# Even-layer input projections of two token groups by seven half-size products, and the forward gated pass as two streams

## The chip, the core and the metric

The kernel runs on one core of one Trainium2 chip. Its engines are TensorE (PE, matrix products into PSUM), VectorE (DVE), ScalarE (ACT), GpSimd (POOL) and SyncE (SP), which here issues all DMA transfers. The metric is device microseconds of the whole program, as the median of several executions; smaller is better. One further execution is recorded by the hardware profiler, and all rows shown come from it.

## What is computed

A two-layer encoder over 2048 prompt tokens and 512 sample tokens, width 1024, in float32. The even layer projects its input once, and two mixers share the projection: gated linear attention (four heads, one scan in each direction, decays that depend on the data) and window attention (eight query heads, two key heads, a bias by distance, a sink logit). The odd layer is a gated convolution of width three. Cut to what matters here:

```python
def even_sublayer(x, w_in, w_up_f, b_f, w_up_b, b_b, norm_g, sink, rel_bias, w_out):
    u = x @ w_in
    qa, ka, va, za, gd, qb, kb, vb, zb = jnp.split(u, _offsets(EVEN_SPLITS), axis=-1)
    ya = gla_mixer(qa, ka, va, za, gd, w_up_f, b_f, w_up_b, b_b, norm_g)
    yb = swa_mixer(qb, kb, vb, zb, rel_bias, sink)
    return jnp.concatenate([ya, yb], axis=-1) @ w_out
...
        x = layer_norm(DN_ALPHA * x + sub, ln_g[l], ln_b[l])
```

## The kernel before

**Precision.** A float32 product is made of three products of a reduced type: every operand is split into a high part and the rest, and high x high, high x rest and rest x high are summed in PSUM. ACT makes the high part with a cast; the rest is a subtraction, on DVE for activations (`prep`, L795) and on POOL for weights (`cook`, `cook_low`, L531 and L545).

**Tiles and stages.** The 2560 tokens form five groups of 512, group 4 being the sample and groups 0 to 3 the prompt; each group holds four chunks of 128. In the even layer's input projection 21 channel tiles of 128 (k: 0 to 3, q: 4 to 7, keys and queries of window attention: 8 to 12, the gates: 13 to 20) are computed per group by `dense_ch` (L569), 24 matmuls of 512 columns each: eight slices of the contraction, three products. Values and the low-rank input of the decays come from `e1_tok` (L1025), 192 matmuls of 336 columns. `e1_ch` (L1071) runs the channel tiles and hands each PSUM bank to `take`, which scales, splits or gates it and stores it to DRAM; for tiles 2 to 9 it also makes one decay each way per head (one matmul, then four functions on ACT and one DVE instruction). The list `stages` in `run` (L2103) fixes the order of the dense work: token projections and channel tiles of group 4, of 3, of 2, of 1, the output projection of group 4 (oe4), then group 0, the odd layer's input projection of group 4 (`odd_one`, called "one"), output projections oe0, oo4, oe1, oe2, and two "pair" stages of the odd layer.

**A stage of seven products exists already.** `odd_pair` (L1944) treats two groups and two channel tiles as a 2 x 2 block product and makes it of seven products of half the contraction (12 matmuls of 512 columns each) rather than eight. `prep_pair` (L909) makes the sums of activation blocks, `pair_weights` (L1858) the sums of weight blocks, and the results are sums of the seven banks, made on DVE.

**Two streams run beside the dense work.** `gla_stream` (L1454) goes through the groups 4, 3, 2, 1, 0. For each chunk `inside` (L1186) does the work within the chunk and the backward scan; when a sequence is through (after group 4, and after group 0) `along` (L1402) makes the forward pass, one step per chunk, each step with its state update, norm, transposes and store. `swa_front` (L1510) and `swa_back` (L1579) do window attention, one block per chunk: scores, bias and softmax in front, products with the values behind. `setup_bias` (L734) loads its bias into two of the four tiles P. A mark such as `gla_in3` or `swa_in3` in `flow.done` tells a stream that a group's inputs are stored; `done_e1_0` says that all of group 0's are. `best` in `swa_front` takes the newest group first, and from `done_e1_0` on the lowest chunk first (L1523).

**The order is written out ahead.** `Flow` and `Model` (L97 and L263) go through the program with estimated times; the dense list drives, and at each pause `pump` (L337) issues the steps of the streams whose data should be ready. Streams have a rank (preparation 0, gated 1, window 2), and `room` (L332) holds them back while DVE or ACT is over 4 or 5 us behind PE by the estimate. Each engine then works through its queue in this fixed order. Where the dense list needs a mark that is not there, `until` (L346) lets the streams go on alone. The output projection of group g waits so, in `out_ln` (L1758), for its `prep`, which waits for `gla`g and for the four blocks of window attention of the group (`mixed`, L2125).

**Tiles.** `st` are eight tiles of 128 x 4 x 512 for split activations (four for a group); `wh`, `wl`, `ws` belong to the weights; `md` (8) and `pr` (3) are general tiles of 128 x 512; P, Q, K0, K1, V, pth, ptl and gb are window attention's; tA, tB, QQ, KK, A, S, km, qn, v are gated attention's. Profile rows give all work the same line, L242, because a helper records it; so tiles tell groups apart.

Of the kernel before, what the change touches and what calls it, by code (L numbers as in the profile page):

```python
# [376 lines left out]
class Trunk:  # L377
    def __init__(self, tc, nc, I, y_out, ctx):
# [35 lines left out]
        self.blocks = []  # L414
# [319 lines left out]
    def setup_bias(self):  # L734
        nc, I, c = self.nc, self.I, self.const
        yield from self.setup_late()
        oh = self.e((32, 512), "gb", bufs=2)
        nc.sync.dma_start(oh[:], I["onehot"])
        ml = self.e((8, 512), "gb", bufs=2)
# [6 lines left out]
        line = self.e((8, 512), "pth", bufs=2)  # L746
# [4 lines left out]
        for h in range(8):  # L751
            rows = self.e((128, 512), "ptl", bufs=2)
            nc.sync.dma_start(rows[:], self.line_s[h:h + 1].broadcast_to([128, 512]))
            yield [rows]
            nc.sync.dma_start(self.bias_s[h], rows[:])
            yield 2.0
        b = self.bias_s
        yield 6.0
        self.bias = [self.new(self.e2, (128, 4, 385), F32, "P", 4, True) for _ in range(2)]
# [265 lines left out]
    def e1_tok(self, g):  # L1025
# [9 lines left out]
        stores = {"gla_in": 24, "swa_in": 29, "done_sw": 33, "done_e1_": 37}  # L1035
# [35 lines left out]
    def e1_ch(self, groups, us):  # L1071
# [3 lines left out]
        if us[0] == 0:  # L1075
            if groups == (4,):
# [25 lines left out]
        def split(g, u, p):  # L1102
            sc = 1.0 if u == 8 else 0.125
            hi, lo = self.m2(dt=F32R), self.m2(dt=F32R)
# [6 lines left out]
            def store():  # L1111
                for i, o in enumerate((hi, lo)):
                    for hh in range(2):
# [4 lines left out]
                        else:  # L1118
                            nc.sync.dma_start(
                                self.qb_s[4 * g:4 * g + 4, 64 * i:64 * i + 64, 2 * (u - 9) + hh].rearrange("c p t -> p c t"),  # L1120
                                s.rearrange("p (c t) -> p c t", c=4))
                self.left[g]("swa_in")
            flow.defer(rest, hi, lo, p)

        def take(g, u, p):
            if u < 8:
# [7 lines left out]
                if u == 0:  # L1134
# [3 lines left out]
                    X = G[g] = self.new(self.yp, (128, 512), F32R, "y", 4, True)  # L1138
# [12 lines left out]
            if 1 < u < 10:  # L1151
                decay(g, (u - 2) // 4, (u - 2) % 4)

        for u in us:
# [7 lines left out]
            if u == 9:  # L1162
                self.drop(up, *(G[g] for g in groups))
                up = self.up = None
                G.clear()
        if u == 16:
            for g in groups:
                self.release("e1_%d" % g)
                flow.mark("end_e1_%d" % g)

# [15 lines left out]
    def inside(self, c, first, last, ld, K, ahead):  # L1186
# [189 lines left out]
        if not last:  # L1376
# [4 lines left out]
            self.flow.defer(lambda: nc.sync.dma_start(self.m_s[c], A[:].rearrange("p h t -> p (h t)")), A)  # L1381
        yield [Q]

    def along_load(self, c, first, last):

        nc = self.nc
        X = self.e((128, 2, 512), ("tA", "QQ")[c % 2])
        nc.sync.dma_start(X[:, 1], self.op_s[c])
        if not first:
            nc.sync.dma_start(X[:, 0], self.qf_s[c])  # L1390
        if c % 2:
            M = None if last else self.e((128, 512), "v")[:]
            ga = self.e((128, 512), "qn")[:]
        else:
            Y = self.e((128, 2, 512), "KK")
            M, ga = Y[:, 0], Y[:, 1]
        if not last:
            nc.sync.dma_start(M, self.m_s[c])
        nc.sync.dma_start(ga, self.ga_s[c])
        return X, M, ga  # L1400
# [804 lines left out]
```

## Time and profile before

| | us |
|---|---|
| median of three runs | 2368.8 |
| lowest and highest of them | 2368.19, 2370.43 |
| the profiled execution | 2370.12 |
| its span, first to last instruction | 2368.1 |

The granted PE clock over the span was 0.998 of full speed. The stages, by their first matmul on PE in the trace: token projections of group 4 from 6.4 us, its channel tiles from 40, group 3 from 165 and 203, group 2 from 372 and 413, group 1 from 587 and 629, oe4 from 804, group 0 from 866 and 902, "one" from 1075, oe0 from 1320, the two pair stages from 1506 and 1914. The span is what lies between the first and the last instruction; the measured time of the same execution is 2.0 us longer. A row by stretches gives, for each engine, its busy time and, behind the x, the number of its instructions. Because matmuls are pipelined, a busy PE says that matmuls were in flight; how many ran in a stretch says how fast.

### The profile page before, as it was taken

Reading aid. Unit: us, or ns where it says so; the run is one execution under the profiler, and the core shown is the slowest. Engines: PE = TensorE matmul, PEld = TensorE weight load, DVE = VectorE, ACT = ScalarE, POOL = GpSimd, SP = SyncE. Lnnn points to the kernel's source line nnn. Section 1 sums busy time; section 2 is a strip of 40 time slices with the busy share of each in tenths; the row PEclk is TensorE's granted clock in tenths of the full one; section 3 lists DMA queues with packets and bytes.
Section 4 is the critical chain, followed back from the end, with each engine's and each line's share of the span. In section 5 each row is a group of like instructions: output and inputs, shape, how many; then the busy total and the mean of one; then the engine's idle time right before and its main releaser. Section 6 shows DMA issues by size and latency. Waiting matters only on the chain.

```text
span 2368.1 us, 43087 instructions
## 1 busy us (share of the span) xinstructions
PE 2343.9 (99%) x15830; PEld 1951.8 (82%) x15830; DVE 1582.8 (67%) x2699; ACT 1226.1 (52%) x2363; POOL 1418.4 (60%) x1610
## 2 busy tenths in 40 slices
PE   8999999999999999999999999999999999999998
PEld 8888889888988888888888888878888877888887
DVE  2267756767767677577776467876566587656567
ACT  4666776656576645665577532543334343333431
POOL 5454435443444444444444467898887689988674
PEclk9999999999999999999999999999999999999999
DMA  7977686676667657675478777232124633221573
GB/s 230 295 226 233 221 269 229 209 221 221 218 194 236 223 173 242 197 218 161 158 245 268 266 261 243 92 116 89 52 78 140 217 105 103 73 72 58 175 242 121
DMA packets 275057, 437.37 MB, mean 185 GB/s; under 512 B 21360, under 2 KB 160240, under 8 KB 274848
## 3 DMA queue, kind: packets, MB, share of 16 engines
q1 hardware_dynamic: 274848, 434.64, 56.5%
q8 instruction: 125, 2.05, 0.4%
q14 instruction: 84, 0.69, 0.1%
HBM read 319.72 MB, written 114.84 MB: 184 GB/s over the span
## 4 chain that ended last, share of the span: by engine, by line
PE 87%; DVE 5%; POOL 4%; DMA 2%; issue 1%; ACT 1%; SPq 0%; POOLq 0%; DVEq 0%; ACTq 0%
PE acc L242 71%; PE ps L242 17%; POOL wl L242 1%; POOL wh L242 1%; DVE st L242 1%; DVE bst L242 1%; DVE y L242 1%; POOL md L242 0%; SPq L242 0%; DVE QQ L242 0%; DVE P L242 0%; DVE KK L242 0%; DMA K<-kb_s 0%; DMA mix_s<-gb 0%; DMA op_s<-QQ 0%
## 5 line engine op out<-in xcount | busy, mean ns | idle before, releaser
L242 POOL TENSOR_TENSOR wl<-ws,wh 128x256 fp32r<-128x256 f32 (+1 forms) x912 | 750.7, 855 | 711.4 <-PE acc L242 478.0
L242 PE MATMUL acc<-st,wh 128*128 128x512 f32 x3160 | 828.5, 395 | 2.8 <-DVE pr L242 2.0
L242 PEld LDWEIGHTS acc<-st,wh 128*128 128x128 f32 x3160 | 580.9, 188 | 121.0 <-issue 3.1
L242 PE MATMUL acc<-st,wl 128*128 128x512 f32 x1744 | 471.9, 395 | 2.8 <-POOL wl L242 1.9
L242 PE MATMUL acc<-wh,st 128*128 128x512 f32 (+1 forms) x1680 | 389.4, 371 | 7.9 <-ACT st L242 6.4
L242 PEld LDWEIGHTS acc<-st,wl 128*128 128x128 f32 x1744 | 320.8, 188 | 68.0 <-POOL wl L242 4.1
L242 PEld LDWEIGHTS acc<-wh,st 128*128 128x128 f32 x1680 | 300.2, 189 | 55.1 <-ACT st L242 6.4
L242 ACT CAST wh<-ws 128x1024 fp32r<-128x1024 f32 (+2 forms) x252 | 249.0, 989 | 184.2 <-DMA ws<-in_w_oo 55.9
L242 PE MATMUL acc<-wl,st 128*128 128x512 f32 (+1 forms) x840 | 209.0, 368 | 0.6 <-POOL wl L242 0.5
L242 ACT ACTIVATE md<-md 128x512 f32<-128x512 f32 x264 | 164.7, 631 | 20.5 <-DVE md L242 14.9
L242 PEld LDWEIGHTS acc<-wl,st 128*128 128x128 f32 x840 | 150.7, 188 | 23.8 <-POOL wl L242 1.3
L242 DVE SCALAR_TENSOR_TENSOR md<-acc,md 128x512 f32<-128x512 f32 (+1 forms) x113 | 77.0, 683 | 81.5 <-ACT md L242 76.5
L242 DVE TENSOR_TENSOR st<-pr,st 128x512 fp32r<-128x512 f32 x115 | 98.5, 874 | 41.6 <-ACT st L242 41.2
L242 ACT ACTIVATE md<-acc 128x512 f32<-128x512 f32 (+1 forms) x133 | 76.2, 597 | 67.0 <-PE acc L242 66.5
L242 POOL TENSOR_TENSOR wh<-md,wh 128x256 fp32r<-128x256 f32 x118 | 96.7, 842 | 13.6 <-ACT wh L242 13.1
L242 ACT CAST pth<-ps 128x512 fp32r<-128x512 f32 x112 | 65.3, 583 | 73.1 <-PE ps L242 72.3
L242 DVE CUSTOM_DVE_ANT_0 P<-ps,P 128x384 f32<-128x384 f32 (+1 forms) x160 | 79.3, 525 | 29.6 <-PE ps L242 29.0
L242 ACT ACTIVATE P<-P,nm 128x385 f32<-128x385 f32 (+1 forms) x160 | 93.2, 587 | 3.9 <-DVE nm L242 3.9
L242 ACT ACTIVATE mv<-mv,eps 128x1 f32<-128x1 f32 x40 | 11.8, 295 | 151.8 <-DVE mv L242 147.7
L242 PE MATMUL acc<-P,wh 128*128 128x512 f32 x312 | 89.5, 400 | 0.4 <-POOL wh L242 0.4
L242 ACT COPY km<-KK 128x512 f32<-128x512 f32 x80 | 50.8, 635 | 72.2 <-DVE KK L242 50.9
L242 ACT CAST st<-pr 128x512 fp32r<-128x512 f32 x115 | 68.3, 617 | 30.3 <-DMA pr<-mix_s 12.9
(490 smaller groups left out, 4090.2 us busy)
## 6 DMA issues: line engine op xcount, KB each, us to landing
ws<-in_w_ch SPq DMA_DIRECT2D x105, 512.0 KB, 4.4
ws<-in_w_od SPq DMA_DIRECT2D x58, 512.0 KB, 4.2
ws<-in_w_oe SPq DMA_DIRECT2D x40, 512.0 KB, 3.8
ws<-in_w_oo SPq DMA_DIRECT2D x36, 512.0 KB, 3.5
K<-kb_s SPq DMA_DIRECT2D x32, 384.0 KB, 6.3
d_s<-md SPq DMA_DIRECT2D x40, 256.0 KB, 4.2
qb_s<-md SPq DMA_DIRECT2D x80, 128.0 KB, 3.9
tA<-d_s SPq DMA_DIRECT2D x20, 512.0 KB, 5.7
```

Source lines behind the costliest of these rows:

```text
L242: r = f(*a, **k)
```

## The change

Groups 4 and 3 are projected together. The order becomes: token projections of both, channel tile 0 of both, then ten units of two channel tiles by `even_pair`, with `prep_even` for the activations' blocks (raw inputs loaded again, four block sums, three of them kept in window attention's tiles and in `md`) and `pair_weights` for the weights' blocks. The decays are made in the first four units; the queries of window attention come in the seventh and eighth unit. The gated stream starts when the tiles that it shares are free ("early", after four units); the bias is loaded after the last unit has released P. The forward pass becomes two streams: `along` makes the output and the next state, `along_back` the norm, transposes, gate and store, up to three chunks behind. All other stages stay.

```diff
         nc, I, c = self.nc, self.I, self.const
         yield from self.setup_late()
-        oh = self.e((32, 512), "gb", bufs=2)
+        yield "up"
+        yield 2.0
+        oh = self.e((32, 512), "QQ")
         nc.sync.dma_start(oh[:], I["onehot"])
-        ml = self.e((8, 512), "gb", bufs=2)
+        ml = self.e((8, 512), "tA")
         nc.sync.dma_start(ml[:], I["mline"])
...
+        for i in (6, 7, 5):
+            yield "free_paire_%d" % i
+        while self.free_at([(self.e2, "P", 4)]) > self.flow.t:
+            yield 0.4
         self.bias = [self.new(self.e2, (128, 4, 385), F32, "P", 4, True) for _ in range(2)]
...
-        stores = {"gla_in": 24, "swa_in": 29, "done_sw": 33, "done_e1_": 37}
+        names = ["gla_in", "swa_in", "done_sw", "done_e1_"] if g < 3 else ["gla_in", "done_e1_", "swa_in", "done_sw"]
+        stores = {n: 24 + sum({"swa_in": 5}.get(x, 4) for x in names[1:i + 1]) for i, n in enumerate(names)}
...
-                    X = G[g] = self.new(self.yp, (128, 512), F32R, "y", 4, True)
+                    X = G[g] = self.take([(self.e2, "v", 1), (self.e2, "qn", 1)] if units else [(self.yp, "y", 4)],
+                                         (128, 512), F32R)
...
+        if units:
+            own = self.owned["e1_%d" % groups[1]]
+            self.drop(*own[:2])
+            del own[:2]
+            flow.mark("plain_e")
+            yield from self.even_pair(groups, units, take, put, decay)
...
+    def prep_even(self, a, b):
+
+        nc, flow = self.nc, self.flow
+        yield "start_e1_%d" % a
+        yield 20.0
+        hi, lo = {}, {}
+        self.pairs["e"] = (hi, lo)
+        e2 = self.e2
+        self.rooms = {n: m for n, m in (("P", 3), ("Q", 2))}
+        homes = [(e2, "P", 4), (e2, "Q", 1), (e2, "pth", 2), (e2, "ptl", 2), (e2, "gb", 2), (e2, "K0", 1), (e2, "K1", 1),
+                 (e2, "V", 1), (self.md, "md", 8)]
...
+        for n in (6, 7, 5):
+            hi[n], lo[n] = [], []
+        self.early = early = [(e2, "S", 2), (e2, "km", 2), (e2, "A", 1), (e2, "tB", 1)]
+        places = early + self.half
+        todo, raws, last = [(k, i, g) for k in range(4) for i in range(2) for g in (a, b)], [], []
...
+        for k in range(4):
+            while len(raws) < 4:
+                get()
+                if len(raws) < 4:
+                    yield 0.4
+            yield raws[:4]
+            while self.free_at(places) > flow.t:
+                yield 0.4
+            b11, b12, b21, b22 = raws
+            t = self.take(places, (128, 512))
+            sub(t[:], b12[:], b11[:])
+            sub(b12[:], b22[:], b12[:])
+            sub(b22[:], b22[:], t[:])
+            sub(b21[:], b21[:], b22[:])
+            self.drop(b11)
+            last.append(b21)
+            raws.clear()
+            yield [b22]
+            for n, r in ((6, b22), (7, b12), (5, t)):
+                hi[n].append(cell())
+                lo[n].append(cell())
+                split(n, k, r, None)
+                yield []
+        yield "plain_e"
+        hi[4], lo[4] = self.big_cells(), self.big_cells()
+        for k, r in enumerate(last):
+            split(4, k, r, None)
+            yield []
+
...
+    def even_pair(self, groups, units, take, put, decay):
+
+        nc, flow = self.nc, self.flow
+        a, b = groups
+        hi, lo = self.pairs["e"]
+        at = lambda c: c[0][:, c[1]]
+        H, L = {}, {}
+        for i, g, o in ((1, a, 0), (2, a, 4), (3, b, 4)):
+            H[i], L[i] = ([f(o + k) for k in range(4)] for f in self.x["e1_%d" % g])
...
+        def after(i, u):
+            c1, c2 = u["ct"]
+            if i == 1:
+                u["s1"] = mid()
+                nc.scalar.copy(u["s1"][:], u[1][:])
+            elif i == 6:
+                flow.force(u[1])
+                u["u1"] = mid()
+                add(u["u1"], u[6], u["s1"])
+            elif i == 7:
+                flow.force(u[6])
+                u["u2"] = mid()
+                add(u["u2"], u[7], u["u1"])
+            elif i == 5:
+                flow.force(u[6])
+                flow.force(u[7])
+                t = mid()
+                add(t, u[5], u["u2"])
+                out(b, c2, t)
+                add(u["u1"], u[5], u["u1"])
+            elif i == 2:
+                flow.force(u[5])
+                t = mid()
+                add(t, u[2], u["s1"])
+                out(a, c1, t)
+                self.drop(u["s1"])
+            elif i == 4:
+                flow.force(u[2])
+                add(u["u2"], u[4], u["u2"])
+                out(a, c2, u["u2"])
+            else:
+                flow.force(u[5])
+                flow.force(u[4])
+                add(u["u1"], u[3], u["u1"])
+                out(b, c1, u["u1"])
+            self.drop(u[i])
+
+        decays = [(g, i // 4, i % 4) for i in range(8) for g in groups]
+        end = len(units) - 1
+        for n, cts in enumerate(units):
+            u = {"ct": cts}
+            for i in (1, 6, 7, 5, 2, 4, 3):
+                if n == 0 and i in (4, 5, 6, 7):
+                    yield "paire_%d" % i
+                if (n, i) == (end - 1, 1):
+                    flow.mark("late_paire")
+                if "wb_e_%d_%d" % (n, i) not in flow.done:
+                    yield "wb_e_%d_%d" % (n, i)
+                if i not in H:
+                    H[i], L[i] = [at(c) for c in hi[i]], [at(c) for c in lo[i]]
+                w = self.wblocks.pop(("e", n, i))
+                p = u[i] = self.pd(hold=True)
+                for k in range(4):
+                    c = slice(k * 128, k * 128 + 128)
+                    nc.tensor.matmul(p[:], w[:, 0, c], H[i][k], start=(k == 0), stop=False)
+                    nc.tensor.matmul(p[:], w[:, 0, c], L[i][k], start=False, stop=False)
+                    yield
+                for k in range(4):
+                    c = slice(k * 128, k * 128 + 128)
+                    nc.tensor.matmul(p[:], w[:, 1, c], H[i][k], start=False, stop=(k == 3))
+                    if k == 1:
+                        yield
+                self.drop(w)
+                flow.defer(lambda i=i, u=u: after(i, u), p)
...
+                if n < 4 and i in (6, 5, 2, 3) and decays:
+                    decay(*decays.pop(0))
+                yield
+            if n == 3:
+                self.drop(self.up, *(self.G[g] for g in groups))
+                self.up = None
+                self.G.clear()
+                flow.mark("early")
+        del self.pairs["e"]
...
+        self.backs.append((c, X))
...
+    def along_back(self):
+        for c in [*range(16, 20), *range(16)]:
+            while not self.backs:
+                yield 0.4
+            _, X = self.backs.pop(0)
+            yield [X]
...
+            if g == 4:
+                yield "early"
+                while any(self.model.spare(*h[1:]) < h[2] for h in self.early + [(self.e2, "qn", 1), (self.e2, "v", 1)]):
+                    yield 0.4
...
+            front, back = {}, {}
+            todo = [list(range(c0, c1)) for _ in range(2)]
+
+            def more(c):
+                if todo[0] and todo[0][0] <= c + 1:
+                    x = todo[0].pop(0)
+                    front[x] = self.along_load(x, *ends(x))
+                x = todo[1][0] if todo[1] else c1
+                if x <= c + 2 and x < c1 and (x < c0 + 3 or "back_%d" % (x - 3) in self.flow.done):
+                    back[x] = self.along_load_back(todo[1].pop(0))
+            more(c0 - 1)
+            for c in range(c0, c1):
+                more(c)
+                while c not in back:
+                    yield 0.4
+                    more(c)
+                ld, X = front.pop(c), back.pop(c)
+                yield [x for x in (*ld, X) if x is not None]
+                yield from self.along(c, *ends(c), ld, X)
+                ld = X = None
             self.sf = None
+            yield "back_%d" % (c1 - 1)
...
-                while self.free_at(self.mids) > flow.t:
+                places = self.mids if p != "e" or n == 0 else self.half + (self.early if n < 4 else self.large)
+                while self.free_at(places) > flow.t:
                     yield 0.3
-                t = sums[name] = self.take(self.mids, (128, 512))
...
-        stages = [("tok", 4), ("ch", ((4,), A + B)), ("tok", 3), ("ch", ((3,), A + B)),
+        even = [(1, 2), (3, 4), (5, 6), (7, 8), (13, 14), (15, 16), (9, 10), (11, 12), (17, 18), (19, 20)]
+        stages = [("tok", 4), ("tok", 3), ("ch", ((4, 3), [0], even)),
...
-        flow.add(self.prep("e1_3", xT(3), ["start_e1_4"]), 60.0, True)
-        flow.add(self.prep("e1_2", xT(2), ["start_e1_3"], then="end_e1_4"), 150.0, True)
-        flow.add(self.prep("e1_1", xT(1), ["start_e1_2"], then="end_e1_3"), 150.0, True)
+        flow.add(self.prep("e1_3", xT(3), ["start_e1_4"], deep=3), 4.0, True)
+        flow.add(self.prep("e1_2", xT(2), ["late_paire"], then="free_paire_1"), 150.0, True)
+        flow.add(self.prep("e1_1", xT(1), ["start_e1_2"]), 150.0, True)
...
+        flow.add(self.pair_weights("e", [tuple(I["w_ch"][u] for u in x) for x in even], 0), 0.0, True)
+        flow.add(self.prep_even(4, 3), 0.0, True)
...
+        flow.add(self.along_back(), rank=1)
```

## What is predicted, before the changed kernel has run

> **What bounds the kernel now.** I read the page's busy times first, then the waits of TensorE (PE), then busy time in stretches cut at the stages. The first fence holds the page's busy line and two of its 40-slice rows, then one line of the view of waits.
>
> ```profile
> PE 2343.9 (99%) x15830; PEld 1951.8 (82%) x15830; DVE 1582.8 (67%) x2699; ACT 1226.1 (52%) x2363; POOL 1418.4 (60%) x1610
> PE   8999999999999999999999999999999999999998
> DVE  2267756767767677577776467876566587656567
> ...
> PE acc L242 <- ACT st L242: 6.4, 1, 6.4
> ```
>
> PE is busy almost everywhere and its one long wait, 6.4 us, is the start. VectorE (DVE) sits near seven tenths from slice 3 to slice 22, where the two attention streams run beside the projections. The next fence is the view by stretches (busy us and instructions of PE, weight loads, DVE, ACT, POOL; granted clock; DMA share and rate).
>
> ```profile
> 0.00:43.00 43.00, 36.40 (x207) 34.11 (x208) 15.52 (x31) 17.23 (x30) 25.52 (x44) 1.00 0.72 230
> 43.00:166.00 123.00, 123.00 (x782) 100.87 (x781) 45.37 (x82) 76.38 (x124) 61.46 (x82) 1.00 0.87 270
> 43.00:366.00 323.00, 323.00 (x2522) 272.12 (x2521) 179.90 (x389) 216.68 (x438) 150.90 (x197) 1.00 0.78 246
> 366.00:475.00 109.00, 108.91 (x1165) 94.01 (x1164) 81.16 (x174) 69.61 (x136) 48.31 (x65) 1.00 0.69 220
> 475.00:527.00 52.00, 52.00 (x588) 42.02 (x587) 38.30 (x76) 31.06 (x56) 26.88 (x30) 1.00 0.73 217
> 527.00:965.00 438.00, 436.85 (x4088) 369.99 (x4088) 315.94 (x663) 264.00 (x519) 189.81 (x244) 1.00 0.67 215
> 965.00:1017.00 52.00, 52.00 (x381) 42.94 (x380) 27.40 (x55) 32.15 (x58) 23.18 (x30) 1.00 0.71 209
> 1017.00:1200.00 183.00, 182.38 (x1692) 149.73 (x1691) 140.56 (x294) 106.70 (x213) 82.77 (x95) 1.00 0.58 186
> 1200.00:1319.00 119.00, 119.00 (x616) 100.44 (x615) 78.50 (x151) 85.68 (x260) 52.17 (x67) 1.00 0.79 261
> 1319.00:1413.00 94.00, 93.83 (x434) 77.77 (x433) 50.63 (x71) 36.36 (x83) 55.42 (x66) 1.00 0.75 259
> 1500.00:1600.00 100.00, 97.00 (x412) 77.67 (x411) 81.40 (x95) 41.97 (x73) 92.28 (x86) 0.98 0.26 90
> 1550.00:1555.00 5.00, 4.07 (x11) 2.93 (x10) 3.93 (x7) 2.34 (x3) 5.00 (x7) 0.66 0.26 105
> 1600.00:1700.00 100.00, 100.00 (x439) 81.98 (x438) 61.29 (x77) 36.52 (x53) 87.81 (x92) 1.00 0.24 79
> ```
>
> From 1600 to 1700 nothing but 512-wide matmuls runs: 100/439 = 0.2278 us each. So the kernel is bound by PE's count of matmuls, as long as the streams arrive in time. How near they are to being late is in the next fence: issues from the views by tile, and one line of the DMA queue's timeline.
>
> ```profile
> L242 SPq DMA_DIRECT2D P<-bias_s x2: 426/467/508, 126.2 to 126.6; - x2
> L242 SPq DMA_DIRECT2D Q<-qb_s x20: 319/332/593, 132.4 to 1186.9; - x20
> L242 SPq DMA_DIRECT2D KK<-k_s x40: 319/423/1602, 109.5 to 1130.7; - x40
> L242 SPq DMA_DIRECT2D mix_s<-gb x20: 524/565/826, 235.8 to 1261.1; - x20
> L242 SPq DMA_DIRECT2D mix_s<-qn x10: 524/525/847, 334.1 to 1358.4; - x10
> 1263.46 1.60 SPq L242 DMA_DIRECT2D pr<-mix_s  x3
> 1319.65 1.17 PE L242 MATMUL acc<-wh,st 128*128 128x512 f32 x4
> ```
>
> Window attention starts 6 us after its bias is loaded, loads its 20 blocks from 132 to 1187, and stores the last at 1261. The output projection of group 0 (oe0) loads its input 2 us later and begins on PE at 1319.7. So its slack is some 50 us. The gated stream's last forward steps (1358) are wanted only by a much later stage.
>
> **The matmuls.** Twenty channel tiles of two groups took 20 x 2 x 24 = 960 matmuls; ten units of seven products of 12 take 840. 120 x 0.2278 = **27.3 us less**. The 21st tile and the token products stay.
>
> **What the units need from the other engines** is priced by these groups of the view by shape.
>
> ```profile
> L242 DVE TENSOR_TENSOR md<-acc,md 128x512 f32<-128x512 f32 x91 | 61.1, 681 | 13.4 <-PE acc L242 11.3 <-ACT md L242 1.3
> L242 DVE TENSOR_TENSOR md<-md,ws 128x512 f32<-128x512 f32 x11 | 13.7, 1244 | 13.0 <-POOL md L242 13.0
> L242 ACT CAST wh<-md 128x512 fp32r<-128x512 f32 x59 | 36.4, 619 | 90.5 <-PE acc L242 41.4 <-DVE md L242 39.2 <-POOL md L242 9.9
> L242 ACT ACTIVATE md<-md 128x512 f32<-128x512 f32 x264 | 164.7, 631 | 20.5 <-DVE md L242 14.9
> L242 POOL TENSOR_TENSOR wl<-md,wl 128x256 fp32r<-128x256 f32 x74 | 60.5, 840 | 5.1 <-ACT wl L242 5.1
> L242 DVE TENSOR_TENSOR st<-pr,st 128x512 fp32r<-128x512 f32 x115 | 98.5, 874 | 41.6 <-ACT st L242 41.2
> ```
>
> A unit lasts 7 x 12 x 0.2278 = 19.1 us on PE. Beside it run: on DVE seven additions, 7 x 0.681 = 4.8 us; on ACT seven casts, 7 x 0.619 = 4.3 us, one copy of about 0.6, and in the first four units four decays of four functions, 16 x 0.63 = 10 us; on POOL 14 subtractions, 14 x 0.84 = 11.8 us, and up to four sums of weights at about 1.24. All fit in 19 us, though POOL reaches 17. The block sums for the activations (prep_even) cost 16 subtractions, 16 casts and 16 more subtractions: 32 x 0.874 = 28 us of DVE, over the first 95 us, where DVE was a third busy (43 to 166: 45 of 123). SiLU and the splits now read both inputs from SBUF, 42 DVE instructions at up to 1.244 instead of 0.681, 24 us at the most, in the same light stretch. I cost all this at nothing; the cover is PE's own 19 us a unit. Twenty weight tiles of 512 KB are loaded once less, 16 inputs of 256 KB once more, all through SP: nothing, at a DMA share that falls from 0.87.
>
> **Friction.** The first difference of weights needs two sums, a cast and two subtractions (2 x 1.24 + 0.62 + 1.68 = 4.8 us) against a slot of 12 x 0.2278 = 2.7 us. The old seven-product stage lost (439 - 412) x 0.228 = 6.2 us in its first 100 us, with DVE at 81%. Bounds 0 and 6.2; DVE is lighter here, so 3. Group 3's token stage moves up to about 43 us, when its input must be split already, and group 2's activations wait for the last unit's buffers: bounds 0 and the 6.4 of the old start; nearer 0, since the loads go on beside a whole stage, so 1. Together **4 us**.
>
> **What moves, and the stall it may bring.** This term decides the sign. The tiles of window attention (P, Q, K0, K1, V, pth, ptl, gb) now hold block sums until the last unit, and the bias is loaded only then. When is that? Start and first token stage 43; the second, 192 of the first's matmuls, 192/207 x 36.4 = 34, so 77; tile 0 for both groups 48 x 0.2278 = 11, so 88; 840 matmuls 191, decays 4, friction 3, so 286. Gated attention starts after four units (about 183) and adds PE time: between 43 and 366 all but 1008 x 0.2278 + 34 + 4 = 268 us was streams', 55 us for four chunks and some four blocks, 7 us each; about 3.3 chunks fit, 23 us. The stage ends near 309 and window attention starts near **315 instead of 132**. Its DVE time by tile (P, ptl, gb in turn; columns as above):
>
> ```profile
> 43.00:366.00 323.00, 12.69 (x84) 10.19 (x84) 34.68 (x76) 25.21 (x90) 0.00 (x0) 1.00 0.78 246
> 366.00:1319.00 953.00, 54.55 (x364) 44.80 (x364) 116.92 (x244) 79.40 (x270) 0.00 (x0) 1.00 0.68 215
> 43.00:366.00 323.00, 7.88 (x20) 3.79 (x20) 13.63 (x20) 0.00 (x0) 1.00 0.78 246
> 43.00:366.00 323.00, 0.00 (x0) 0.00 (x0) 5.48 (x8) 4.65 (x8) 5.66 (x4) 1.00 0.78 246
> ```
>
> By 366, where the old group 3 is done, 34.7 + 13.6 + 5.5 = 54 us of it were over; the new kernel has done none. Gated attention is behind by about half a chunk and four forward steps, some 20 us of DVE (an estimate: a chunk each 45 us at two fifths of DVE is 18). To be done from 315 until the output projection of group 1 (oe1), for which all blocks of groups 0 and 1 are wanted: the old 366 to 1413, 81 + 38 + 316 + 27 + 141 + 79 + 51 = 733, plus 54 + 20 = **807 us**. Without a stall oe1 comes at 1413 - 23 = 1390, 1075 us later: DVE must be **75.1%** busy. With both streams at work it was 81.2/109 = 74.5% (366 to 475), 315.9/438 = 72.1% (527 to 965), 140.6/183 = 76.8% (1017 to 1200). At 76.8% the work takes 1051 us and nothing waits; at 74.5% 1083, **8 us late**; at 72.1% 1119, 44 late. Below zero the term can't go, since PE has its matmuls to do. I take 74.5%, the row nearest to what is needed. The waiting instruction is the first matmul of oe0 or oe1 (dense stream, at out_ln); behind it stand all dense matmuls, while the streams' own go on.
>
> The two-stream forward pass changes no instruction's size; it lets a step's state update run ahead of its norms. Its end gates nothing before (1358 against a stage beyond 1750), so 0; it is cover for the later start of the gated stream (183 against 110), which has the tiles to itself until 315 and so catches up.
>
> **Sum**: -27.3 + 4 + 8 = -15.3 us. Against the profiled execution (span 2368.1, 2370.1 with what lies around it, and 2368.8 the median, 0.7 over the span) that is 2352.8 of span and **2353.5** on the medians' scale.
>
> **A rule on the clock.** In the row 1550 to 1555 the granted clock was 0.66 and 11 matmuls took 4.07 us of busy time, where full rate gives 18: 7 x 0.228 = 1.6 us lost behind short gaps. If each stall at an output stage costs as much again, two stalls bring 3 us: 2356.5, inside the forecast's own range and part of its chance. The Trainium skill (TensorE: Matmul & The Clock Gate, "What's actually happening") has the array fall to half rate after an idle window of about 3.4 us; by that a long wait at oe0 costs more than its length. The trace agrees only in part: the dip came behind gaps of about 1 us in all, and the opening wait of 6.4 us shows a clock of 1.00.
>
> **Rivals.** (a) *The streams catch up whole*: DVE at 76.8% as in 1017 to 1200. For it: it has been reached with projections beside. Against: only late, where POOL is light. -27.3 + 4 = 2345.5. (b) *DVE becomes the bound and PE waits at oe0 and oe1*: DVE stays at 72.1%, the longest row. 44 us late: -27.3 + 4 + 44 = +20.7, **2389.5, slower**. It decides from a stall of 23.3 us on, that is from a mean share under 807/1098 = 73.5%; the three rows together give 537.7/730 = 73.7%, so this is close. (c) *The gain is just given back*: a stall of 19 to 28 us, or units that lose 6.2 us in each 100 as at 1500 (another 13 us): 2364 to 2373.5. (d) The change doesn't do what it says: the tile count is in the code, so this has no chance of its own.
>
> **How the numbers follow.** Forecast, a stall of up to some 18 us: 0.35, own range 2347 to 2364. (a) 0.16, (c) 0.16, (b) 0.33. A measurement of this kernel can tell about 0.2% (4.7 us) from no change: faster 0.35 + 0.16 = 0.51, same 0.16, slower 0.33. The range 2342 to 2390 leaves out the far half of (b) and a little below (a).
>
> **What would show it.** Right: group 3's projections end near 310; the first Q load at about 315; DVE between 315 and 1390 at 74 to 76%; PE idle under 10 us before oe0 and oe1; the pure stretch beyond 1500 unchanged but some 15 us earlier. Wrong: PE gaps inside the units (weights late: POOL; banks late: DVE), a stage end beyond 320, or PE idle of over 23 us ahead of oe0 or oe1 with the last mix store just before it. If oe0's wait ends on a forward step's store, my reading that the gated stream keeps up is wrong.

## The result, and the profile after

The changed kernel takes **2435.1 us** (median of four runs, 2433.0 to 2441.1) against 2369.5 for the kernel before on the same chip: ratio 1.028, interval 1.026 to 1.030. It is slower by 66 us, where 15 us faster was forecast and 2390 was the upper end of the range. The profiled execution after has a span of 2434.5 us.

First the page of the kernel after, its busy line and three rows of 40 slices.

```profile
PE 2357.3 (97%) x15710; PEld 1949.2 (80%) x15710; DVE 1677.5 (69%) x2817; ACT 1236.8 (51%) x2410; POOL 1461.0 (60%) x1610
...
PE   8899989999999999999996899999999999999998
...
DVE  4659874775677765777776675885656588656567
...
PEclk9999989999999999999998899999999999999999
```

120 matmuls are gone (15830 to 15710), yet PE is busy 13 us longer: the granted clock over the span was 0.984 instead of 0.998, some 34 us (an estimate from these two shares). PE is no longer full in slices 2 and 6 and, deeper, in slices 22 and 23 (1278 to 1400 us). The view by stretches, cut at the end of "one", at the first matmul of oe0 and at the first of the first pair stage, first before (a cut at 315 added), then after, from the end of group 3's stage on (columns as in the prediction):

```profile
315.00:1319.30 1004.30, 1002.44 (x8784) 842.71 (x8782) 711.07 (x1482) 632.81 (x1357) 445.46 (x558) 1.00 0.68 217
1319.30:1506.10 186.80, 186.34 (x873) 155.09 (x872) 118.44 (x155) 73.60 (x149) 125.73 (x138) 1.00 0.70 235
1506.10:2368.10 862.00, 846.70 (x3713) 691.17 (x3711) 587.09 (x716) 329.12 (x513) 693.11 (x705) 1.00 0.34 115
```

```profile
326.80:1281.00 954.20, 944.25 (x8569) 792.17 (x8567) 671.41 (x1423) 571.94 (x1147) 431.73 (x524) 0.99 0.64 207
1281.00:1334.80 53.80, 36.32 (x178) 27.68 (x176) 36.03 (x97) 34.17 (x127) 4.02 (x5) 0.81 0.71 222
1334.80:1571.20 236.40, 222.97 (x1042) 183.54 (x1043) 159.39 (x258) 115.55 (x297) 125.06 (x137) 0.96 0.74 242
1571.20:2434.50 863.30, 848.42 (x3713) 691.13 (x3711) 589.17 (x716) 329.61 (x513) 692.30 (x705) 1.00 0.34 114
```

The reader is to see three things. The stretch from the pair stages on is the same, 862 and 863 us with the same 3713 matmuls. The dense list reaches the end of "one" 38 us *earlier* (1281 against 1319). Between the two, what took 187 us takes 290: a wait of 54 us ahead of oe0, and four output stages in 236 us instead of 187. So -38 + 103 + 1 = +66.

What fills that stretch is told by the stores of the two streams that are still to come when "one" ends (the view by tile of `mix_s`, from there on; gated forward steps are stored from KK, qn, tA or QQ, window blocks from gb). Before:

```profile
L242 SPq DMA_DIRECT2D mix_s<-KK x2: 525/525/525, 1321.6 to 1346.1; - x2
L242 SPq DMA_DIRECT2D mix_s<-qn x2: 524/524/524, 1332.5 to 1358.4; - x2
```

After:

```profile
L242 SPq DMA_DIRECT2D mix_s<-tA x6: 524/524/597, 1300.3 to 1421.2; - x6
L242 SPq DMA_DIRECT2D mix_s<-QQ x5: 524/525/559, 1306.4 to 1406.4; - x5
L242 SPq DMA_DIRECT2D mix_s<-KK x5: 525/526/567, 1317.6 to 1417.1; - x5
L242 SPq DMA_DIRECT2D mix_s<-gb x4: 524/542/566, 1315.6 to 1430.7; - x4
```

Four forward steps were left before; now all 16 of the prompt and four window blocks are. oe0 has to wait for the first four of the forward steps. When the streams load their inputs (views by tile, after):

```profile
L242 SPq DMA_DIRECT2D Q<-qb_s x20: 319/326/725, 320.7 to 1347.3; - x20
L242 SPq DMA_DIRECT2D KK<-k_s x40: 319/430/847, 179.9 to 1237.9; - x40
```

And the end of the wait, in the timeline of the DMA queue and then of PE:

```profile
1324.93 0.52 SPq L242 DMA_DIRECT2D mix_s<-tA  x1
1329.50 1.37 SPq L242 DMA_DIRECT2D pr<-mix_s  x3
```

```profile
1334.77 0.49 PE L242 MATMUL acc<-wh,st 128*128 128x512 f32 x1 [0.96 <-ACT st L242]
```

Gated attention starts 70 us later than before and loads its last backward chunk 107 us later; window attention starts 188 later and loads its last block 160 later. oe0's inputs are loaded 4.6 us after the forward step of chunk 3 is stored (1324.9), while the last window block stored before that went out at 1315.6: the wait ends on the gated stream.

### The profile page after: what moved, and what is told of

The parts are those of the page before. It is cut to its first block, busy times and chain, and to the rows that moved or that the text cites. A ratio compares the mean times of both kernels' runs of the same rounds, so it can differ in the third digit from the quotient of the medians.

```text
span 2434.5 us, 43056 instructions
## 1 busy us (share of the span) xinstructions
PE 2357.3 (97%) x15710; PEld 1949.2 (80%) x15710; DVE 1677.5 (69%) x2817; ACT 1236.8 (51%) x2410; POOL 1461.0 (60%) x1610
## 4 chain that ended last, share of the span: by engine, by line
PE 75%; DVE 7%; POOL 3%; DMA 3%; issue 2%; ACT 1%; SPq 1%; POOLq 0%; DVEq 0%; ACTq 0%
PE acc L242 59%; PE ps L242 16%; POOL wl L242 2%; DVE st L242 1%; POOL wh L242 1%; DVE md L242 1%; DVE KK L242 1%; DMA K<-kb_s 1%; DVE y L242 1%; DVE QQ L242 1%; SPq L242 1%; DVE bst L242 0%; POOL md L242 0%; ACT km L242 0%; DVE P L242 0%
## 5 line engine op out<-in xcount | busy, mean ns | idle before, releaser
L242 POOL TENSOR_TENSOR wl<-ws,wh 128x256 fp32r<-128x256 f32 (+1 forms) x752 | 630.5, 870 | 534.5 <-PE acc L242 306.6
L242 PE MATMUL acc<-st,wh 128*128 128x512 f32 x2808 | 737.8, 395 | 2.1 <-DVE pr L242 2.0
L242 PEld LDWEIGHTS acc<-st,wh 128*128 128x128 f32 x2808 | 516.5, 188 | 108.8 <-issue 4.1
L242 PE MATMUL acc<-st,wl 128*128 128x512 f32 x1616 | 433.7, 396 | 2.1 <-POOL wl L242 2.1
L242 ACT CAST wh<-ws 128x1024 fp32r<-128x1024 f32 (+2 forms) x218 | 210.8, 967 | 143.9 <-DMA ws<-in_w_oo 42.4
L242 ACT ACTIVATE md<-md 128x512 f32<-128x512 f32 (+1 forms) x288 | 179.5, 631 | 27.3 <-DVE md L242 21.4
L242 POOL TENSOR_TENSOR gb<-gb 128x512 f32<-128x512 f32 x20 | 27.3, 1363 | 198.9 <-DVE gb L242 198.9
L242 PE MATMUL acc<-P,wh 128*128 128x512 f32 x420 | 121.9, 402 | 0.7 <-POOL wh L242 0.7
L242 DVE TENSOR_TENSOR md<-acc,md 128x512 f32<-128x512 f32 (+1 forms) x133 | 82.8, 633 | 21.8 <-PE acc L242 16.3
L242 PEld LDWEIGHTS acc<-P,wh 128*128 128x128 f32 x420 | 79.8, 191 | 21.2 <-POOL wh L242 2.7
L242 ACT ACTIVATE md<-acc 128x512 f32<-128x512 f32 (+1 forms) x97 | 56.7, 596 | 72.1 <-PE acc L242 67.2
```

The lines of the kernel that those rows point to most:

```text
L242: r = f(*a, **k)
```

## The experiments

Theories: **S**, the streams start late and cannot catch up; **F**, the two-stream forward pass costs by itself; **D**, VectorE's load holds them, against **R**, their order and their own chains of steps do; **W** and **N**, it is the order written out ahead (which stream comes first; or any departure from the order before); **U**, the units themselves lose; **K**, the low clock behind waits is a price of its own. Beside each result, in brackets: the end of "one", the stream stores left then (forward steps + window blocks), and the length of the stretch from there to the first pair stage. Before: 1319, 4 + 0, 187 us; after: 1281, 16 + 4, 290 us.

**One part of the change alone, in the kernel before.** The bias of window attention held back, the gated stream held back, both, and the new forward pass:

```diff
 # b_late_window, in setup_bias
+        yield "start_e1_3"
+        yield 150.0
 # b_late_gated, in gla_stream (b_late_both: both edits)
+            if g == 4:
+                yield "start_e1_3"
+                yield 14.0
 # b_two: along, along_load_back, along_back and the second half of gla_stream as in the change
```

> The kernel before, with one line more: the bias of window attention is loaded only 150 us after group 3's token stage has begun (about 315 us instead of 126), so this stream starts as late as in the changed kernel; all products as before. Theory S (the streams set the time: what window attention loses by its late start isn't caught up before the output projections of groups 0 and 1): 25 to 45 us slower, with PE idle ahead of oe0. Theory U (the loss lies in the seven-product units and the hand-over behind them, before 400 us): within 5 us of before. Theory F (the two-stream forward pass costs the time): within 5 us.

Measured 2399.5, +30 us (1286, 10 + 4, 251 us). As S expected.

> The kernel before, with the gated stream alone held back to about 180 us (instead of 110); window attention starts at 132 as before. S: 10 to 40 us slower, as the gated stream has no slack either and its group 0 store comes later. My forecast's own reading, that the gated stream catches up: within 5 us. U and F: within 5 us.

Measured 2397.7, +28 (1308, 11 + 0, 224 us). The stream started 63 us later and loaded its last backward chunk 66 us later, at 1197: at this order it catches up nothing, and this reading of the forecast is wrong.

> The kernel before, with both streams held back, gated to about 180 us and window to about 315, as in the changed kernel, and all 960 matmuls of the eight-product form. S: 65 to 95 us slower, about what the change lost (66) plus the 27 us of matmuls that it saved; a gap ahead of oe0 of 40 us or more, ended by a store of group 0's attention. U and F: under 10 us slower.

Measured 2449.5, +80 (1270, 16 + 5, 317 us), as S expected. No unit of seven products is in this kernel, and it has the wait of the changed one. Its view by stretches:

```profile
1269.80:1320.20 50.40, 34.49 (x179) 26.83 (x177) 37.78 (x97) 32.05 (x116) 5.48 (x6) 0.84 0.67 213
1320.20:1587.20 267.00, 236.47 (x1091) 192.51 (x1092) 172.24 (x292) 126.16 (x335) 121.85 (x137) 0.92 0.68 227
```

> The kernel before with the second part of the change alone: forward pass as two streams, everything else as before. F: 20 us slower or more, and the changed kernel with the old forward pass would win that back. S: within 8 us, as the forward pass gates nothing while the streams are on time.

Measured 2405.1, +36 (1311, 11 + 0, 234 us). S fails here: the gated stream starts on time (112) and yet loads its last backward chunk at 1203, 73 us later than before. F had it right, but see below.

**One part taken out of the changed kernel, or its order changed.**

```diff
 # a_one: along, along_load and gla_stream as before the change
 # a_nonorm, in swa_front: the softmax isn't divided by its sum
-                    nc.vector.tensor_scalar(Pt[:, h, :w], Pt[:, h, :w], den[:, h:h + 1], None, op0=ALU.mult)
 # a_rank, in run
-        flow.add(self.swa_front())
-        flow.add(self.swa_back())
+        flow.add(self.swa_front(), rank=1)
+        flow.add(self.swa_back(), rank=1)
 # a_oo4_first, in stages (and the gates of prep)
-  ("one", range(8)), ("oe", 0), ("oo", 4),
+  ("one", range(8)), ("oo", 4), ("oe", 0),
```

> The changed kernel with the forward pass of gated attention as one stream again (loads, step, normalization and store of one chunk in a row, one chunk loaded ahead); the units of seven products stay. Changed kernel 2435, kernel before 2369. S (the 66 us come from the two attention streams that start 48 and 190 us later and have no slack left to catch up): the forward pass is the same work, so the time stays within 12 us of 2435. F (the two-stream forward pass costs by itself, as it did alone: +36): 2395 to 2415, and the wait ahead of oe0 shrinks.

Measured 2463.4, 28 *slower* than the changed kernel (1283, 16 + 5, 316 us). F fails, and so does S, which allowed 12 us: what cost 36 us in the one kernel gains 28 in the other.

> The changed kernel without the 320 multiplications on VectorE that divide the softmax of window attention by its sum (the output is not normalized; some 160 us of VectorE over the whole kernel's 20 chunks are left out, 320 instructions of about 0.5 us). D (VectorE's load is what holds the two late streams back): the streams end 50 us or more earlier, the 54 us of wait ahead of oe0 all but go, and the time falls to 2350 to 2385. R (the streams are held by the order in which they are written out and by their own chains of steps, VectorE is only 70% busy): less than 25 us of it come back, 2410 to 2435.

Measured 2403.2, -32 (1309, 12 + 2, 234 us). DVE's busy time fell by 72 us (160 instructions of 0.44 us; the expectation had both numbers too high). Between D and R: with 72 us less to do VectorE was busy only 66% from the units' end to the end of "one" (649 of 981 us), so its load is a part of what paces the streams, not all of it.

> The changed kernel with window attention at the same rank as gated attention when the order is written out, so that of the two the step that is ready first comes first, instead of gated ahead of window. All instructions stay. W (what is lost depends on which of the two streams is put first, since one waits at oe0 for the later of them): a change of more than 15 us in either direction; the wait ahead of oe0 then ends on window attention if gated attention has become earlier, or the other way round. S alone (both streams have the same total lateness, in whatever order): within 15 us of 2435.

Measured 2410.4, -25 (1304, 15 + 2 with a third block stored just as "one" ends, 244 us). No instruction differs, so the order alone is worth this much, as W had it; but the wait ahead of oe0, now 31 us, still ends on the gated stream (chunk 3 stored at 1319.7, the inputs loaded at 1325.9).

> The changed kernel with the stage oo4, which needs only group 4's odd layer, put ahead of oe0 instead of behind it. All instructions stay. S with a wait that is decided at oe0: oo4's 128 wide matmuls a tile, some 43 us, fill the 54 us ahead of oe0, and the time falls by 15 to 40 us. Rival (the time is set by when the streams end, and they run only at the pace that TensorE leaves them): the wait moves behind oo4 or to oe1 and pair0, and the time stays within 12 us of 2435.

Measured 2453.3, +18 (1267, 16 + 5, 325 us). The rival came nearer, though it allowed 12 us: the wait isn't filled but moved. The stretch starts 14 us earlier and is 35 longer.

**What is order, and what is the change?** After a_rank, b_two and a_one the suspicion N had to be tested: edits that change nothing but the order, made to both kernels. "rank" is the edit of a_rank; "five" is

```diff
-    AHEAD = ((5.0, 5.0), (4.0, 4.0), (4.0, 4.0))
+    AHEAD = ((5.0, 5.0), (5.0, 5.0), (5.0, 5.0))
```

> The kernel before with window attention at the same rank as gated attention when the order is written out (the edit of a_rank, made to the kernel before). All instructions, products and stream starts stay; only the order in which the steps are written out differs. N (the kernel before has an order in which streams and dense work happen to end together, and any new order loses that, whatever work is changed): 20 to 45 us slower than 2369, and a_rank (2410) lies within 20 us of it, so that at this order the change itself costs little. S (late starts are what costs): within 12 us of 2369, and the change costs 35 us or more at this order too.

> The kernel before with one number of the written-out order changed: a step of a side stream is let in while VectorE and ScalarE are up to 5 us ahead instead of 4. All instructions stay. N: 15 to 45 us slower than 2369, by waits ahead of or inside the four output stages after the stage one. S and F (only late starts or the two-stream forward pass cost): within 12 us of 2369.

> The changed kernel with the same number changed from 4 to 5 us. S: as far above b_five as the changed kernel is above the kernel before, 66 us, within 15. N: the distance to b_five differs from 66 us by more than 20, in either direction, because each order places its waits anew.

> The kernel before with the two-stream forward pass and with window attention at the same rank. F (the two-stream forward pass costs by itself, +36 as measured at the old rank): 25 us or more above b_rank. N (that +36 was the price of any new order, not of the two streams): within 15 us of b_rank, above or below.

> The kernel before with the two-stream forward pass and 5 us instead of 4. To be set against b_five (2386). F (the two streams cost by themselves, +36 at the old order): 25 us or more above b_five. N (as at equal ranks, where it was +9): within 15 us of b_five.

> The kernel before with both attention streams held as in b_late_both (gated to about 175 us, window attention to about 315 us), and with window attention at the same rank. To be set against b_rank (2396). S (a late start costs what it cost at the old order, 81 us, of which nothing is the order's): 60 us or more above b_rank. N (most of the 81 was the price of leaving the order of the kernel before): less than 25 us above b_rank. Between the two, late starts and order share it.

> The kernel before with both streams held in the same way, and with 5 us instead of 4 in the written-out order. To be set against b_five (2386). S: 60 us or more above b_five. N: less than 25 us above it.

Medians in us, with the distance to the kernel before *at the same order*:

| | old order | rank | five |
|---|---|---|---|
| before | 2369 | 2396 | 2386 |
| + two-stream forward pass | 2405 (+36) | 2405 (+9) | 2408 (+22) |
| + both streams late | 2450 (+80) | 2415 (+19) | 2443 (+57) |
| changed kernel | 2435 (+66) | 2410 (+14) | 2469 (+82) |

By what was expected, b_rank, b_five, b_two_rank and b_late_both_rank came out as N had it; b_two_five, b_late_both_five and a_five lie between N and the other theory.

N is right as far as it goes: the kernel before loses 29 and 18 us (against the 2367.6 of their own runs; ratios 1.012, 1.011 to 1.014, and 1.008, 1.006 to 1.010) by edits that touch no work, so its own order is a good fit. But the late start costs at all three orders (19 to 80), and so does the whole change (14 to 82, about 54 on the mean). The sign is the change's; of the size, more than half can be the order's. F's +36 shrinks to +9 and +22 and turns to a gain in the changed kernel, so no price of its own can be given for the forward pass.

Late starts less the 27 us of matmuls give +53, -8 and +30 at the three orders, against +66, +14 and +82 for the whole change. So the late starts are most of the loss at the old order, less than half of it at "five" and none at "rank"; the other 13, 22 and 52 us belong to units, forward pass and order together, and no run parts them. Nor is a late start passed on whole at every order. Held by 191 to 195 us, window attention loads its last block 168, 126 and 137 us later than at the same order without the hold; the gated stream, held by 60 to 62 us, loads its last backward chunk 101, 36 and 48 us later.

**Is it the units?** The gated stream held until the last unit is over:

```diff
-                yield "early"
+                yield "free_paire_3"
```

> The changed kernel with gated attention held back until the last unit is over (about 325 us) instead of the fourth (180 us). It tells where the 31 us of idle TensorE in the first 400 us and the low clock there come from. U1 (the units and gated attention beside them share VectorE, 92% busy from 180 to 255 us, and TensorE waits for it): idle TensorE up to 400 us falls to 20 us or less. U2 (the units themselves, their start and the hand-over of the input tiles to tok2): it stays within 6 us of 31. In both the streams are 145 us later still, so S gives a total 30 us or more above 2435; a total at or below 2435 would speak against S.

Measured 2472.0, +37 (1283, 16 + 2, 326 us), slower by over 30 us as S expected. Gated attention starts at 286, 106 us later and not 145, window attention at 287, 34 us earlier. In the view by stretches, the last units without gated attention beside them and group 2's token stage behind, first a_hold, then the changed kernel:

```profile
180.00:286.60 106.60, 106.60 (x467) 87.39 (x466) 68.46 (x92) 64.78 (x111) 75.20 (x84) 1.00 0.51 147
286.60:356.40 69.80, 54.57 (x637) 48.82 (x636) 57.54 (x122) 35.62 (x78) 27.29 (x33) 0.85 0.64 213
```

```profile
180.00:255.00 75.00, 69.53 (x711) 54.73 (x710) 69.07 (x92) 43.09 (x75) 59.38 (x57) 1.00 0.51 157
326.80:385.70 58.90, 49.55 (x422) 46.03 (x421) 38.43 (x96) 35.19 (x88) 19.53 (x29) 0.88 0.69 222
```

With the stream away the units run without a gap; beside it PE idles 5.5 of 75 us and DVE is 92% busy. So from 180 us on the units alone aren't short of anything. But the idle time only moves to where the streams begin, and up to 400 us it is 28 us instead of 31: U1 is wrong on the sum, right on the place.

**Is the low clock a price of its own?** Filler transposes where the dense list waits (`warm` is called in `until` before PE's estimated time is moved on); a_rank_warm is the same edit on a_rank:

```diff
+    def warm(self, until):
+        t = self.trunk
+        while t.const_ready and until - self.t > 0.13 and t.free_at([(t.acc, "acc", 4)]) <= self.t:
+            t.nc.tensor.transpose(t.new(t.acc, (128, 512), F32, "acc", 4)[:, :128], t.ident[:], t.ident[:])
```

> The changed kernel with 332 filler transposes of the identity, whose results nobody reads, in the places where TensorE waits for a stream or a block (38 ahead of the first unit, 16 at tok2, 278 ahead of oe0). Nothing else is moved. K (the low granted clock behind a wait is a price of its own, 34 us of the changed kernel, and a TensorE kept busy doesn't pay it): the clock between 1281 us and the start of oe0 rises from 0.81 to 0.93 or more, idle TensorE in the whole kernel falls by 20 us or more, and the time falls by 8 to 25 us. K0 (the streams' chains on VectorE and ScalarE set the end of the wait, the clock only goes along): within 6 us of 2435, or slower, since filler stands in the streams' way on TensorE.

> a_rank (the changed kernel with window attention at the same rank, 2410) with the same filler, 234 transposes. K: 5 to 18 us below 2410, less than in a_warm as its wait ahead of oe0 is shorter; still slower than the 2369 of the kernel before, since the 38 us of the first 400 us and the late streams stay. K0: within 6 us of 2410, or slower.

Measured 2434.6 (1283, 16 + 4, 292 us) and 2413.8 (1307, 15 + 3, 244 us): nothing, and +3. The same wait in the view by stretches of a_warm, and the stages behind it:

```profile
1283.30:1338.50 55.20, 54.66 (x456) 52.43 (x454) 36.41 (x99) 34.29 (x128) 4.04 (x5) 1.00 0.68 223
1338.50:1575.00 236.50, 222.51 (x1043) 182.90 (x1044) 160.72 (x256) 114.88 (x297) 125.74 (x137) 0.96 0.74 240
```

PE is full, the clock is 1.00 instead of 0.81, and the wait lasts 55.2 us instead of 53.8. K falls for this wait: idle PE and low clock were signs of it, not its price. What ends it are steps of the streams: in the changed kernel PE's longest idle times there end on loads (4.17 us on A, 3.90 on K) and on VectorE (2.35). The filler left the clock at 0.97 up to 400 us and at 0.96 behind oe0, so K isn't tested there.

No version beat the kernel before; of those that compute everything, the best with the change is a_rank.

## Why the prediction was wrong

- **The matmuls, -27.3: right.** 120 fewer, and at the same pace (467 in 106.6 us, 0.228 each, in the units of a_hold); the stretch behind the output stages is unchanged.
- **Starts of the streams: nearly right.** Gated 180 (183 forecast), window 321 (315), end of group 3's stage 327 (309).
- **The stall, 8 us: this is the step that failed.** The need stood: 807 us of DVE were forecast from 315 to oe1, and up to 1478, where oe1 begins (1413 plus the 65 us by which the pair stages are later; an estimate), 809.6 were done. The pace did not. It had to be 75.1% and was 69.6% (row below). I picked 74.5%, the row *nearest to the need*, out of rows chosen for both streams being at work. From about 315 to the end of "one" DVE was busy 711/1004 = 70.8% before, and 671/954 = 70.4% after: in this kernel being late didn't make the streams faster. At 70.4% the same sum gives 807/0.704 = 1146 us, oe1 at 1461 instead of 1390, 71 us late, and -27.3 + 4 + 71 = +48: the right side, and most of the size. Why the pace is 70% and not more was not settled: a_nonorm shows that DVE's work is in it, a_rank (713/978 = 72.9%) that the order is.

```profile
315.00:1478.00 1163.00, 1122.14 (x9485) 934.77 (x9485) 809.60 (x1705) 690.31 (x1514) 494.61 (x597) 0.98 0.67 214
```

- **"Gated attention catches up": wrong,** shown by b_late_gated and by the wait at oe0, which ended on a forward step, as the prediction named for this error. At "rank" it does make up 24 of 60 us.
- **Forward pass at 0: not supported.** By itself +9 to +36, within the changed kernel -28 at one order. That its end gates nothing holds for the kernel before only; here its first four steps are what oe0 waits for.
- **Friction, 4 us: too small.** Up to 400 us PE idles 31 us; 7 were there before, nearly all at the start, 5.5 are at the first unit, the rest mostly where streams meet the units and group 2's token stage. The clock was 0.97 there instead of 1.00, some 12 us more (an estimate). What it costs was not isolated: a_warm filled 6 us of the idle time and won nothing.
- **The clock, 3 us: the wrong kind of term.** The Trainium skill (TensorE: Matmul & The Clock Gate, "What's actually happening") has the array drop to half rate after an idle window, by which I said that a wait costs more than its length. The trace shows the drop (0.81 ahead of oe0), but a_warm removes it there and wins nothing. The two rows that I set against the Trainium skill there were misread. The dip at 1551 came behind gaps of 1.14 and 0.94 us, 2.1 us in all, and the 1.00 of the opening is no measurement: the trace's clock records begin at 12.0 us, and up to there the kernel before ran at about half the pace, 15 matmuls of 336 columns in 4 us against 28 just behind:

```profile
8.00:12.00 4.00, 4.00 (x15) 3.93 (x15) 2.12 (x4) 3.24 (x6) 1.89 (x3) 1.00 1.06 375
13.00:17.00 4.00, 4.00 (x28) 4.00 (x27) 2.12 (x3) 2.56 (x4) 3.12 (x5) 1.00 0.94 344
```

- **Rivals.** Of (b) the waits of PE at the output stages are what happened, on the side and by the share that I had named (under 73.5%); its row, 72.1%, was still too high and its 2389.5 too low. That DVE itself is the bound isn't shown: 72 us less of its work won back 32. Against (a) I said that POOL was light from 1017 to 1200; it was 45% busy there (82.8 of 183 us) and 43% from 527 to 965, so that was no argument. The order as a cause of tens of us was not among the rivals, and should have been: every edit here writes the order anew.

## What to carry to other kernels

Where the end is a fixed stage behind streams, count what the streams have left when the independent dense work runs out: in 20 profiles of this kernel the time was the end of "one", plus a stretch that mostly grew with that backlog (4 + 0 steps 187 us, 11 + 0 224 to 234, 16 + 4 290 to 297, 16 + 5 316 to 325), plus 858 to 865 us. The count isn't all: 17 or 18 steps took 244 us in a_rank and a_rank_warm, but 326 in a_hold, where the prompt's first forward step was stored at 1358 instead of 1296 (a_rank). Take the pace of a stream from its whole length, not from its best stretches, and expect a late start to arrive late at the end, if not always by as much, unless a trace shows it catching up. Where a list scheduler writes the order, compare a change at several orders before giving any part of it a price.

## What the runs showed of the hardware

The clock fell behind short stretches in which PE was less than about half busy; no long gap was needed. Two gaps of the kernel after, in PE's timeline (idle time in brackets), and the 10 us behind each:

```profile
216.50 0.69 PE L242 MATMUL ps<-QQ,KK 128*64 128x64 f32 x16 [1.41 <-DVE QQ L242]
...
253.70 0.46 PE L242 MATMUL ps<-QQ,km 128*32 128x32 f32 x32 [2.15 <-DVE QQ L242]
```

```profile
216.00:226.00 10.00, 8.43 (x54) 6.81 (x55) 10.00 (x15) 8.03 (x15) 8.15 (x8) 1.00 0.31 108
253.00:263.00 10.00, 9.04 (x106) 6.76 (x107) 9.41 (x16) 1.25 (x2) 6.63 (x7) 0.83 0.66 203
```

0.83 over 10 us is 1.7 us lost where PE is the bound (an estimate), and just what 3.4 us at half rate would give; the trace's clock records have half rate from 255.11 us for 3.41 us. In the 3.41 us ahead of that PE was busy for 1.41 us, and 0.87 ahead of the next drop, at 296.07; around the gap that brought no drop it was 2.00:

```profile
251.70:255.11 3.41, 1.41 (x36) 1.24 (x37) 3.41 (x4) 0.12 (x1) 3.41 (x4) 1.00 0.91 270
292.66:296.07 3.41, 0.87 (x60) 0.75 (x46) 3.31 (x6) 2.44 (x5) 2.42 (x4) 1.00 0.00 0
214.15:217.56 3.41, 2.00 (x23) 1.39 (x22) 3.41 (x5) 2.63 (x5) 3.41 (x4) 1.00 0.89 264
```

Cut into steps of 3.41 us on the clock records, the full-rate stretches of the 20 profiles say the same: half rate followed all 144 steps with PE busy under 44%, none of 13369 above 80%, and 34 of the 275 between. The Trainium skill (TensorE: Matmul & The Clock Gate, "What's actually happening") has steps of that length and rate, but after an idle window as long; here 2.0 us of idle in 3.41 were enough, and at 1551 in the kernel before 2.1 us in two gaps. Where a wait upstream is the bound, as ahead of oe0, the low clock costs nothing (2434.6 us without it, 2435.1 with it).
